# A two-layer diffusion block on one core: the late modulation sums at a chunk's end moved behind its last tail, two value tiles turned later, and the pairs' copies reordered

## The chip, the cores and the metric

The kernel runs on one core of a Trainium2 chip. The metric is the device time of one execution in microseconds (us). Five engines work side by side, each through its own list of instructions in a fixed order: TensorE (PE in the profile), VectorE (DVE), ScalarE (ACT), GpSimd (POOL) and SyncE (SP). Here POOL and SP mostly issue DMA transfers. An instruction that has to wait holds up everything behind it on its engine.

## The reference

Two layers over 512 latent tokens and 256 context tokens, width 1024. Layer 0 has latent attention and two-dimensional neighbourhood attention side by side, layer 1 grouped-query attention in a sliding window. Each attention and each feed-forward block reads a modulated, normalised stream, and its result goes back through a gate. The modulation vectors are products of a condition vector with a large matrix:

```python
for l in range(DEPTH):
    sh_a, sc_a, g_a, sh_f, sc_f, g_f = jnp.split(silu_c @ mod_w[l] + mod_b[l], 6, axis=-1)
    ...
    a_lat = modulate(h_lat, sh_a, sc_a)
    ...
    h_lat = h_lat + g_a * o_lat
    h_lat = h_lat + g_f * swiglu(modulate(h_lat, sh_f, sc_f), ffn_w_gate_up[l], ffn_w_down[l])
    if ctx_out:
        h_ctx = h_ctx + cg_a * o_ctx
        h_ctx = h_ctx + cg_f * swiglu(modulate(h_ctx, csh_f, csc_f), ffn_w_gate_up[l], ffn_w_down[l])
return rms_norm(h_lat, final_norm)
```

`swiglu` is `(silu(g) * u) @ w_down` with `g, u` the halves of `h @ w_gate_up`; the hidden width is 2816, which is 22 panels of 128.

## The kernel before, in words

Every 32-bit product is made of three TensorE products of split operands: each operand has a head (`wh`, `h`) and a remainder (`wl`, `lo`), and `mm3` and `product` issue head by head, head by remainder, remainder by head. A weight tile is loaded into `wr` by SP (L134), cast to `wh` by ACT (L309, L1518) and its remainder `wl` is made on the DVE (L311, L1519). Activations are kept with 128 features on the partitions and 768 tokens (512 latent, 256 context) along the row.

**The feed-forward block of layer 0** goes through the 22 hidden panels in chunks of four, four, four, four, four and two (`CHUNKS`, numbered 0 to 5). A panel is a `Pair`: `head`, `body` and `tail` are groups of products (a seven-product scheme for the four of a gate and an up panel), and its weights are split on the DVE at L1555 to L1565 and L1519. In the program the head of a pair comes ahead of the tail of the pair before. After the chunk's last tail, which makes the hidden tile `hs[3]` (L1594, then its split by L1518 and L1519), the chunk's down product runs over eight output tiles m = 0 to 7 (`down0`): it loads the residual tile m from memory (`fetched`, L1345, a transfer that POOL issues: `p<-home`), multiplies the weights by the four hidden tiles into two PSUM banks (latent and context part), adds the products to the residual tile on the DVE (L1341) and stores the tile (L1713, POOL: `home<-p`). The buffers of tag `p` hold these residual tiles, among others; there are eight.

PSUM has eight banks, three with tag `s`, two `t`, two `d`, one `o`. `PG` hands them out in the order s, t, s, d, t, s, d, so in the profile `pss`, `pst`, `psd` name the bank of a product. A product that begins a new use of a bank waits for the last reader of the use before, in the down product for an L1341.

**The late modulation sums.** Layer 1's modulation vectors are computed during layer 0's feed-forward, a tile at a time (`late_mods`): POOL fetches a 128 x 1024 weight tile into the only `rope0` buffer (L263), and the DVE multiplies it with the condition vectors and sums (L274, one or two instructions a tile). `late_step(place)` issues the sums of the tile that has been fetched, not ahead of the instruction `place`, and then the fetch of the next tile, which needs the buffer and so waits for the sums. `LATE` says how many such steps go with each pair and each output tile.

**What sets the order.** The program's text gives the order of issue, but a scheduler with its own costs then orders each engine's list; `behind(a, b)` makes it keep a behind b. So moving one step in the text can move others.

**Two other places.** In layer 0's attention `split_pair` takes the raw queries and keys of a neighbourhood pair apart into heads and remainders for two heads; halves of 64 partitions are moved by SP's copies (`t1[up] <- t0[dn]` and so on; L134). In layer 1, `VS` gets the values with tokens on the partitions: six transposes (L1771), four of latent and two of context tiles, of `v32` (made by ACT, L770), and copies. They run among the products of `swa_queries(1)` to `swa_queries(6)`.

## Time and profile before

| | before |
|---|---|
| time, median of 3 runs | 1530.44 us (1529.15 to 1530.89) |
| profiled execution: time, span | 1530.38 us, 1528.6 us |
| granted TensorE clock | 0.998 of full speed |
| busy: PE, DVE, ACT, POOL | 1512.8, 1177.6, 759.9, 194.8 us |
| chain that ended last: PE, DVE, all others | 91%, 5%, 4% |
| DMA | 225.94 MB, mean 148 GB/s |

How to read the rows. A row of the time-line begins with the start of an instruction (or of a run of like ones) and its duration in us, then engine, line, operation, `out<-in` by tile names without their numbers, the shape, and in brackets how long its engine stood idle before it and what ended that. A DMA row shows the time of its issue on the engine that issues it; when it lands is another view.

### The profile page before, as it was taken

The numbers are of one execution on the slowest core, as the hardware profiler recorded it, in microseconds if no ns is written. First come the engines' busy times: TensorE is split into PE (matmuls) and PEld (weight loads), VectorE is DVE, ScalarE is ACT, GpSimd is POOL, SyncE is SP. The second block draws the span as 40 slices with busy tenths as digits, with TensorE's granted clock in tenths as the row PEclk, the third lists the DMA queues.
The fourth block names the chain that finished last, engine by engine and source line by source line (L and its number), as shares of the span: only waits on it lengthen the run. The fifth ranks groups of instructions, "written<-read, shape, count | busy, mean of one in ns | idle before, by whom it ended". The sixth has DMA issues, their size and how long they took to land.

```text
span 1528.6 us, 26556 instructions
## 1 busy us (share of the span) xinstructions
PE 1512.8 (99%) x10008; PEld 1366.8 (89%) x10008; DVE 1177.6 (77%) x2427; ACT 759.9 (50%) x1531; POOL 194.8 (13%) x266
## 2 busy tenths in 40 slices
PE   9999999999999999999999999999999999999997
PEld 7788887889998998999999998888789999899897
DVE  4799877786876786877768677799977779678685
ACT  5533776684654242432424335567857455355353
POOL 0022210000111102012021122460011000000001
PEclk9999999999999999999999999999999999999999
DMA  9675753244733636547375494110224224324232
GB/s 337 242 226 183 182 126 98 58 148 151 234 125 108 232 102 218 183 144 286 122 259 182 151 369 141 60 38 1 98 82 140 84 79 136 104 83 131 90 97 84
DMA packets 80929, 225.94 MB, mean 148 GB/s; under 512 B 11232, under 2 KB 18400, under 8 KB 80800
## 3 DMA queue, kind: packets, MB, share of 16 engines
q1 hardware_dynamic: 61968, 148.73, 30.3%
q0 software_dynamic: 17680, 73.94, 14.2%
q8 instruction: 78, 1.28, 0.3%
q10 hardware_dynamic: 1152, 1.57, 0.3%
q14 instruction: 51, 0.42, 0.1%
HBM read 186.97 MB, written 23.07 MB: 137 GB/s over the span
## 4 chain that ended last, share of the span: by engine, by line
PE 91%; DVE 5%; ACT 1%; issue 1%; DMA 1%; POOL 0%; DVEq 0%; SPq 0%; ACTq 0%; POOLq 0%
PE pss L1532 5%; PE pss L1531 5%; PE pss L1533 5%; PE pss L346 4%; PE pss L349 4%; PE pss L348 4%; PE pso L576 4%; PE psd L346 4%; PE psd L348 4%; PE psd L349 4%; PE pst L346 3%; PE pst L348 3%; PE pst L349 3%; PE pst L1533 3%; PE pst L1532 3%; PE pst L1531 3%
## 5 line engine op out<-in xcount | busy, mean ns | idle before, releaser
L309 ACT CAST wh<-wr 128x512 fp32r<-128x512 f32 (+2 forms) x141 | 109.1, 787 | 211.3 <-DMA wr<-in_w_dn_dram 39.5
L311 DVE TENSOR_TENSOR wl<-wr,wh 128x512 fp32r<-128x512 f32 (+2 forms) x138 | 123.2, 899 | 87.9 <-ACT wh L309 83.5
L583 ACT ACTIVATE p<-p,sm 128x512 f32<-128x512 f32 (+3 forms) x144 | 105.1, 731 | 30.2 <-DVE sm L587 29.4
L1531 PE MATMUL pss<-b,wh 128*128 128x384 f32 (+1 forms) x346 | 107.8, 311 | 0.0
L1532 PE MATMUL pss<-b,wh 128*128 128x384 f32 (+1 forms) x346 | 107.7, 311 | 0.0
L1533 PE MATMUL pss<-b,wl 128*128 128x384 f32 (+1 forms) x346 | 107.2, 311 | 0.0
L274 DVE CUSTOM_DVE_ANT_0 p<-rope,cond 128x1024 bf16<-128x1024 f32 x64 | 78.0, 1219 | 10.6 <-DMA rope<-in_mod_w_dram 10.4
L348 PE MATMUL psd<-b,wh 128*128 128x512 f32 (+2 forms) x245 | 85.3, 348 | 0.0
L576 PE MATMUL pso<-ph,b 128*64 128x256 f32 (+1 forms) x400 | 77.8, 351 | 0.4 <-DVE ph L521 0.4
L576 PE MATMUL pso<-pl,b 128*64 128x256 f32 (+1 forms) x400 | 76.8, 351 | 0.0
L346 PE MATMUL psd<-b,wh 128*128 128x512 f32 (+2 forms) x206 | 75.5, 366 | 0.1
L349 PE MATMUL psd<-b,wl 128*128 128x512 f32 (+2 forms) x206 | 74.6, 362 | 0.0
L1518 ACT CAST wh<-wr 128x1024 fp32r<-128x1024 f32 x39 | 41.0, 1052 | 60.3 <-PE pss L348 15.2
L1531 PE MATMUL pst<-b,wh 128*128 128x384 f32 (+1 forms) x226 | 70.6, 312 | 0.0
L1532 PE MATMUL pst<-b,wh 128*128 128x384 f32 (+1 forms) x226 | 70.5, 312 | 0.0
L1533 PE MATMUL pst<-b,wl 128*128 128x384 f32 (+1 forms) x226 | 70.4, 312 | 0.0
L1518 ACT CAST wh<-pl 128x512 fp32r<-128x512 f32 x78 | 45.1, 619 | 48.5 <-PE pss L1532 21.1
L348 PE MATMUL pss<-b,wh 128*128 128x256 f32 (+2 forms) x215 | 68.9, 320 | 0.0
L346 PE MATMUL pss<-st,wh 128*128 128x512 f32 (+2 forms) x195 | 66.5, 341 | 0.2 <-ACT wh L309 0.2
L349 PE MATMUL pss<-st,wl 128*128 128x256 f32 (+2 forms) x195 | 66.5, 341 | 0.0
L1532 PEld LDWEIGHTS pss<-b,wh 128*128 128x128 f32 x346 | 65.0, 188 | 0.6 <-DVE wl L1519 0.4
L1531 PEld LDWEIGHTS pss<-b,wh 128*128 128x128 f32 x346 | 65.0, 188 | 0.6 <-issue 0.4
(712 smaller groups left out, 5221.4 us busy)
## 6 DMA issues: line engine op xcount, KB each, us to landing
wr<-in_w_gu_dram SPq DMA_DIRECT2D x88, 512.0 KB, 4.1
rope<-in_mod_w_dram POOLq DMA_DIRECT2D x48, 512.0 KB, 3.8
wr<-in_w_dn_dram SPq DMA_DIRECT2D x73, 256.0 KB, 2.8
wr<-in_w_out_dram SPq DMA_DIRECT2D x32, 512.0 KB, 3.6
p<-home POOLq DMA_DIRECT2D x40, 384.0 KB, 6.1
home<-p POOLq DMA_DIRECT2D x40, 384.0 KB, 5.5
wr<-in_w_in_dram SPq DMA_DIRECT2D x21, 512.0 KB, 3.9
ph<-in_mod_w_dram SPq DMA_DIRECT2D x24, 256.0 KB, 3.1
```

What stands on the lines that cost most here:

```text
L274: behind(V.tensor_tensor_reduce(out=unused, in0=w, in1=cond[:, v, :], op0=ALU.mult, op1=ALU.add, scale=1.0, scalar=0.0, accum_out=MOD[l, c ...
L309: behind(S.copy(h, r), *after[:1])
L311: behind((G if eng else V).tensor_tensor(lo, r, f(h), op=ALU.subtract), *after[1:])
L346: ins = PE.matmul(o, wh[:, k], mh[:, c], start=first and k == 0, stop=False)
L348: PE.matmul(o, wh[:, k], ml[:, c], start=False, stop=False)
L349: marks["product"] = PE.matmul(o, wl[:, k], mh[:, c], start=False, stop=last and k == n - 1)
L576: ins = PE.matmul(o[64 * i : 64 * i + 64, c], v(kt), t, start=n == 0, stop=n == len(moving[i]) - 1)
L583: S.activation(p[:, c], p[:, c], AF.Exp, bias=nm, scale=-1.0, accum_out=dn)
L1518: S.copy(h, t)
L1531: behind(PE.matmul(o, wh, xh, start=first and k == 0, stop=False, skip_group_check=not first), *after)
L1532: PE.matmul(o, wh, xl, start=False, stop=False, skip_group_check=not first)
L1533: ins = PE.matmul(o, wl, xh, start=False, stop=k == 3, skip_group_check=not first)
```

## The change

Three edits, in the text of the kernel.

1. In `ffn`, for layer 0 and the last pair of a chunk, the one late step that stood behind the pair's body is now behind its tail, and its sums may not be ahead of the tail's last split. This concerns chunks 1 to 4.
2. The transposes of the two context tiles into `VS` are issued after the steps that `swa_queries(2)` brings, behind the last product issued by then.
3. In `split_pair` the copy `t1[up] <- t0[dn]` is issued ahead of the subtraction that makes `lo`, and the two copies of a key tile's upper half onto its lower half come after all four copies into the second head's tiles.

```diff
@@ split_pair
         t0, t1 = sets[p][0]
         S.copy(t0[:, :NT], q)
         lo = q.bitcast(F32R)
+        behind(dma(t1[up, :NT], t0[dn, :NT]), *placed)
         low = V.tensor_tensor(lo, q, f(t0[:, :NT]), op=ALU.subtract)
         up_low(2, low)
         yield
-        behind(dma(t1[up, :NT], t0[dn, :NT]), *placed)
         dma(t1[dn, :NT], lo[dn])
         dma(t0[dn, :NT], lo[up])
...
         for x, y in ((h0, h1), (l0, l1)):
             dma(y[up, :NT], x[dn, :NT])
-            dma(y[dn, :NT], x[dn, :NT])
-            placed[:] = [dma(x[dn, :NT], x[up, :NT])]
+            placed[:] = [dma(y[dn, :NT], x[dn, :NT])]
+        for x in (h0, l0):
+            behind(dma(x[dn, :NT], x[up, :NT]), *placed)
         yield
@@ ffn
-            hs, last = [], None
+            hs, last, held_back = [], None, False
...
                     p.body()
                     hs.append(p.dst)
                     last = p
-                    if more(j) > 0:
+                    held_back = l == 0 and j == k0 + kc - 1 and more(j) > 0
+                    if more(j) > 0 and not held_back:
                         late_step(p.done)
...
             elif last:
                 last.tail()
+            if held_back:
+                late_step(last.done)
@@ layer 1
-    for t0, n in ((0, 4), (4, 2)):
+
+    def swa_values(t0, n, *after):
         o = PS("t")
         for i in range(n):
-            PE.transpose(o[:, i * P : (i + 1) * P], v32[:, (t0 + i) * P : (t0 + i + 1) * P], ident)
+            behind(PE.transpose(o[:, i * P : (i + 1) * P], v32[:, (t0 + i) * P : (t0 + i + 1) * P], ident), *after)
         copy(VS[:, t0 * P : (t0 + n) * P], o[:, : n * P])
+
+    swa_values(0, 4)
...
     for p in range(1, 7):
         beside(swa_queries(p))
...
+        if p == 2:
+            drain(side_work[0])
+            step(3)
+            swa_values(4, 2, marks["product"])
```

In the lists that follow, lines of the changed kernel are one to four higher than before (L1341 becomes L1342, L1345 L1346, L1713 L1717). Names carry their numbers.

SP at the copies of pair 3, where `st_2103` and `st_2104` are the query heads' tiles, `st_2105` to `st_2108` the keys' and `p_1646` is `lo`; before:

```order
L134 DMA b_1857<-b_1857 64x768
L134 DMA b_1858<-b_1858 64x768
L134 DMA st_2104<-st_2103 64x768
L134 DMA st_2104<-p_1646 64x768
L134 DMA st_2107<-st_2105 64x768
L134 DMA st_2103<-p_1646 64x768
L134 DMA st_2107<-st_2105 64x768
```

and now:

```order
L134 DMA b_1857<-b_1857 64x768
L134 DMA st_2104<-st_2103 64x768
L134 DMA b_1858<-b_1858 64x768
L134 DMA st_2104<-p_1646 64x768
L134 DMA st_2103<-p_1646 64x768
L134 DMA st_2107<-st_2105 64x768 x2
```

The first query copy moves ahead by one place, and the two copies from `p_1646` stand together.

POOL at the end of chunk 2, where `home_4240` to `home_4244` are residual tiles 0 to 4 in memory and each `p` the tile in the chip; before:

```order
L1345 DMA p_7409<-home_4240 128x768
L263 DMA rope_1532_7369<-in_mod_w_dram 128x1024
L1345 DMA p_7444<-home_4241 128x768
L1345 DMA p_7481<-home_4242 128x768
L263 DMA rope_1540_7442<-in_mod_w_dram 128x1024
L1713 DMA home_4240<-p_7409 128x768
L1713 DMA home_4241<-p_7444 128x768
L1345 DMA p_7522<-home_4243 128x768
L1345 DMA p_7559<-home_4244 128x768
L1713 DMA home_4242<-p_7481 128x768
```

and now:

```order
L1346 DMA p_7409<-home_4240 128x768
L263 DMA rope_1535_7407<-in_mod_w_dram 128x1024
L1717 DMA home_4240<-p_7409 128x768
L1346 DMA p_7444<-home_4241 128x768
L1346 DMA p_7481<-home_4242 128x768
L263 DMA rope_1540_7442<-in_mod_w_dram 128x1024
L1717 DMA home_4241<-p_7444 128x768
L1717 DMA home_4242<-p_7481 128x768
L1346 DMA p_7522<-home_4243 128x768
L1346 DMA p_7559<-home_4244 128x768
```

The loads of tiles 1 and 2 stand behind the store of tile 0, and those of tiles 3 and 4 behind the stores of tiles 1 and 2. Chunks 3 and 4 read the same with other numbers.

The DVE a little later in the same chunk, where `p_7522` and `p_7559` are tiles 3 and 4, and L1555 to `pl_7747` split the next pair's weights; before:

```order
L311 TENSOR_TENSOR wl_7686<-wr_7683,wh_7685 128x512
L1341 SCALAR_TENSOR_TENSOR p_7522<-pss_7524,mod_1136_5144,p_7522 128x512
L1341 SCALAR_TENSOR_TENSOR p_7522<-psd_7525,mod_1137_5145,p_7522 128x256
L1341 SCALAR_TENSOR_TENSOR p_7559<-pst_7561,mod_1136_5144,p_7559 128x512
L1341 SCALAR_TENSOR_TENSOR p_7559<-pss_7562,mod_1137_5145,p_7559 128x256
L1555 TENSOR_TENSOR pl_7730<-wr_7719 128x512
L1557 TENSOR_TENSOR ph_7731<-pl_7730,wr_7718 128x512
L1561 TENSOR_TENSOR ph_7736<-wr_7718,wr_7719 128x512
L1519 TENSOR_TENSOR wl_7723<-wr_7718,wh_7722 128x1024
L1565 TENSOR_TENSOR pl_7742<-wr_7718,ph_7731 128x512
L1519 TENSOR_TENSOR pl_7747<-wr_7719,ph_7746 128x512
```

and now:

```order
L1556 TENSOR_TENSOR pl_7730<-wr_7719 128x512
L1558 TENSOR_TENSOR ph_7731<-pl_7730,wr_7718 128x512
L1562 TENSOR_TENSOR ph_7736<-wr_7718,wr_7719 128x512
L1566 TENSOR_TENSOR pl_7742<-wr_7718,ph_7731 128x512
L1520 TENSOR_TENSOR wl_7723<-wr_7718,wh_7722 128x1024
L1520 TENSOR_TENSOR pl_7747<-wr_7719,ph_7746 128x512
L1342 SCALAR_TENSOR_TENSOR p_7522<-pss_7524,mod_1136_5144,p_7522 128x512
L1342 SCALAR_TENSOR_TENSOR p_7522<-psd_7525,mod_1137_5145,p_7522 128x256
L1342 SCALAR_TENSOR_TENSOR p_7559<-pst_7561,mod_1136_5144,p_7559 128x512
L1342 SCALAR_TENSOR_TENSOR p_7559<-pss_7562,mod_1137_5145,p_7559 128x256
```

The residuals of tiles 3 and 4 stand behind the six weight splits. The residuals of tiles 1 and 2 (not shown) moved likewise behind the L311 of tile 6's weights.

## The prediction

> **What bounds the kernel now.** I read the page's first part, then the time-line of each engine around the places that the change touches. The page's head and its busy times:

> ```profile
> span 1528.6 us, 26556 instructions
> PE 1512.8 (99%) x10008; PEld 1366.8 (89%) x10008; DVE 1177.6 (77%) x2427; ACT 759.9 (50%) x1531; POOL 194.8 (13%) x266
> ```

> TensorE runs its products in a fixed order and is busy for 99% of the span. The number of products does not change (only places in the order do), so the time can change only by waits: those that vanish from TensorE's row, and new ones. Each part below is therefore one question: what does TensorE wait for there now, and what after?

> **Part 3, the pairs' copies: about -0.7 us.** SP's time-line around pair 3, then the DVE instruction and the product that wait:

> ```profile
> 173.86 0.54 SPq L134 DMA_DIRECT2D st<-st  x1
> ...
> 181.51 0.46 SPq L134 DMA_DIRECT2D st<-p  x1
> ```
> ```profile
> 187.82 0.69 DVE L587 CUSTOM_DVE_ANT_0 p<-pss,b 128x512 f32<-128x512 f32 x1 [2.29 <-PE pss L778]
> ```
> ```profile
> 188.58 0.39 PE L777 MATMUL pss<-b,b 128*128 128x256 f32 x1 [0.78 <-DVE sm L587]
> ```

> The last `st<-p` copy reads `lo`, a tile with tag `p`; L587 writes its next row into a tile with that tag, and it starts at 187.82 although the DVE has been free for 2.29. (The row names a product; I take the copy, issued 6.3 us before, to be what ends last.) That copy could not be issued before the `st<-st` of 173.86 had landed, since it overwrites the half that this one reads. The change issues that `st<-st` one row earlier on SP (a row there takes about 0.5 us) and drops the row between the two `st<-p` copies. So the chain moves forward by 0.5 us at least, and at most the whole 0.78 of the product's wait goes. I take 0.7. If the copies don't move, the gain is 0.

> **Part 1 at chunk 1's end: about -0.9 us.** DVE's time-line, then the product:

> ```profile
> 592.97 1.23 DVE L274 CUSTOM_DVE_ANT_0 p<-rope,cond 128x1024 bf16<-128x1024 f32 x1 [0.79 <-DMA rope<-in_mod_w_dram]
> ...
> 595.05 1.22 DVE L274 CUSTOM_DVE_ANT_0 p<-rope,cond 128x1024 bf16<-128x1024 f32 x1
> ...
> 596.67 1.22 DVE L1519 TENSOR_TENSOR b<-p,b 128x384 fp32r<-128x384 f32 x2
> ```
> ```profile
> 596.30 0.27 PE L346 MATMUL pst<-b,wh 128*128 128x256 f32 x1
> 597.27 0.39 PE L348 MATMUL pst<-b,wh 128*128 128x256 f32 x1 [0.70 <-DVE b L1519]
> ```

> Two sums of 1.2 us each, the first after 0.79 of waiting for its weights, stand ahead of the split (L1519) of the chunk's last hidden tile, for which the first down product waits. The product before it began at 596.30; these two follow each other in 0.12 where nothing waits (a 256-column product, by the rows of this place), so 0.85 is lost. With the sums behind the split, the split comes some 2 us earlier: the wait goes, -0.9. The products that use the last hidden tile wait for nothing new here, as chunk 1's first three `home` loads are issued ahead of the rope fetch in either order.

> **The rest of the order: -0.3 and 0.** Three waits of TensorE, at the last chunk, at layer 1's value tiles, and 19 us behind these:

> ```profile
> 933.08 0.40 PE L349 MATMUL psd<-st,st 128*128 128x512 f32 x1
> 933.65 0.50 PE L346 MATMUL pst<-st,nb 128*128 128x512 f32 x1 [0.17 <-ACT st L1518]
> ```
> ```profile
> 979.35 0.44 PE L1771 MATMUL pst<-ident_r,b 128*128 128x128 f32 x2 [0.45 <-ACT b L770]
> ```
> ```profile
> 998.08 0.28 PE L777 MATMUL pss<-st,st 128*128 128x256 f32 x1
> 998.46 0.50 PE L346 MATMUL psd<-b,wh 128*128 128x512 f32 x1
> ```

> At 933.65 the scheduler now puts eight more products in front of the waiting one; the distance to the product before it is 0.57 us, of which a 512-column product needs some 0.23, and the rest goes: -0.3. At 979.35 the transposes of the context tiles wait for L770; ten products later (10 x 0.23 = 2.3 us) they don't, which is worth 0.45 to 0.62. But the product at 998.46, the first of a new psd bank, starts 0.38 after its neighbour and follows an ACT, DVE and POOL chain that does not wait for these transposes. What TensorE gains at 979 it waits for at 998: I take 0 and keep -0.6 as the other end.

> Gains together: 0.7 + 0.9 + 0.3 = 1.9 us.

> **Part 1 at the ends of chunks 2, 3 and 4: about +9.6 us.** Here the same move reorders POOL's queue. POOL's time-line at chunk 2, and what the loads took there:

> ```profile
> 683.00 1.08 POOL L1345 DMA_DIRECT2D p<-home  x2
> ...
> 692.95 0.55 POOL L1713 DMA_DIRECT2D home<-p  x1 [0.22 <-issue]
> 695.20 0.55 POOL L1713 DMA_DIRECT2D home<-p  x1 [1.71 <-DVE p L1341]
> 695.74 1.08 POOL L1345 DMA_DIRECT2D p<-home  x2
> ```
> ```profile
> DMA to landing us min/median/max: 4.2/5.5/7.3
> ```

> Before, the loads of residual tiles 1 and 2 go out at 683.00, far ahead. After, they stand behind the fetch that waits for the late sum, and behind the store of tile 0, which waits for tile 0's residual (issued at 692.95 here). They go out at about 693 and land, by the row's 4.2 to 7.3, at 697 to 700. The DVE follows suit; its time-line before, and two products:

> ```profile
> 693.77 0.74 DVE L1341 SCALAR_TENSOR_TENSOR p<-pss,mod,p 128x512 f32<-128x512 f32 x1
> ...
> 698.99 0.69 DVE L311 TENSOR_TENSOR wl<-wr,wh 128x512 fp32r<-128x512 f32 x1 [1.15 <-ACT wh L309]
> ...
> 702.62 0.75 DVE L1341 SCALAR_TENSOR_TENSOR p<-pss,mod,p 128x512 f32<-128x512 f32 x1 [0.17 <-DMA p<-home]
> ...
> 706.58 0.69 DVE L1555 TENSOR_TENSOR pl<-wr 128x512 f32<-128x512 f32 x1 [1.77 <-DMA wr<-in_w_gu_dram]
> ...
> 710.86 1.22 DVE L274 CUSTOM_DVE_ANT_0 p<-rope,cond 128x1024 bf16<-128x1024 f32 x1
> ```
> ```profile
> 699.61 0.28 PE L346 MATMUL pss<-st,wh 128*128 128x256 f32 x1
> ...
> 708.02 0.28 PE L346 MATMUL pss<-st,wh 128*128 128x256 f32 x1
> ```

> First wait. Tile 1's residual (693.77) moves behind the L311 of 698.99, which ends at 699.68; with 0.74 for itself it ends at 700.4. It frees the pss bank that the product at 699.61 (tile 4, third pss after it in the ring) begins: up to 0.8 us of waiting, none if the loads are quick and TensorE is late anyway.

> Second wait, the larger. The residuals of tiles 1 and 2 end near 702, so their stores and then the loads of tiles 3 and 4 go out near 702.5 instead of 695.74 and land at 707 to 710. In the DVE's new order the residual of tile 3 (702.62 now) stands behind the split of the next pair's weights, L1555 up to the row ahead of the L274 at 710.86. So it starts at 710.86 and ends at 711.6. It frees the bank of the pss product that begins at 708.02 (tile 6). That product begins 3.6 us late (the first wait is contained in this). The same two rows at chunks 3 and 4:

> ```profile
> 803.66 1.22 DVE L274 CUSTOM_DVE_ANT_0 p<-rope,cond 128x1024 bf16<-128x1024 f32 x1
> ```
> ```profile
> 800.45 0.28 PE L346 MATMUL pss<-st,wh 128*128 128x256 f32 x1
> ```
> ```profile
> 896.20 1.22 DVE L274 CUSTOM_DVE_ANT_0 p<-rope,cond 128x1024 bf16<-128x1024 f32 x1
> ```
> ```profile
> 892.87 0.28 PE L346 MATMUL pss<-st,wh 128*128 128x256 f32 x1
> ```

> 803.66 + 0.74 - 800.45 = 3.95 and 896.20 + 0.74 - 892.87 = 4.07. Sum 11.6 us, if the split of the weights stays where it is. That hangs on when the gate weights land: L1555 starts on their landing. Their transfer at chunk 2, the DMA share there, and the page's median for such loads:

> ```profile
> DMA to landing us min/median/max: 6.9/6.9/6.9
> ```
> ```profile
> DMA  9999999999979999999798999999999999999999
> ...
> DMA packets 698, 2.84 MB, mean 406 GB/s; under 512 B 101, under 2 KB 101, under 8 KB 698
> ```
> ```profile
> wr<-in_w_gu_dram SPq DMA_DIRECT2D x88, 512.0 KB, 4.1
> ```

> The engines are full there, so the load takes 6.9 and not 4.1. Its issue does not move (it follows the L311 of 698.99). After the change, two stores and two loads of 384 KB move from 695 to 697 to about 701 to 703, and two loads of that size come in at 693: some 0.4 to 0.8 MB less ahead of the gate weights, but as much more beside them. Lower end: 4.1, that is 2.8 us earlier, leaves 0.8, 1.2 and 1.3, together 3.3. Upper end: the 0.79 MB that used to land at 683 to 688 is now in the full stretch, which moves 406 GB/s, so 1.9 us more at each chunk: 11.6 + 5.7 = 17.3 in all. I take 0.65 off each wait, near the measured row: 2.9 + 3.3 + 3.4 = 9.6.

> [...]

> **The sum.** The profiled execution took 1530.38 us (span 1528.6 and 1.8 around it), 0.06 under the median of 1530.44. 1530.4 - 1.9 + 9.6 = 1538.1 us.

> **The rivals.**
> - Light: the gate weights land in 4.1 us, and the waits shrink to 3.3 in all: 1530.4 - 1.9 + 3.3 = 1531.8. For it: the page's median. Against it: the stretch was full at all three chunks.
> - Hidden, the other side: the residual of tile 3 never holds TensorE. The point that decides: the gate weights landing within 6.9 - 3.6 = 3.3 us of their issue, and tile 3's load by then too. Then only gains are left: 1530.4 - 1.9 = 1528.5, and 1527.9 with the 0.6 of the value tiles kept. Against it: 3.3 is below the page's median for that load.
> - Crowded: POOL's late loads also delay the weights: up to 1530.4 - 1.9 + 17.3 = 1545.8.
> - The value tiles do nothing: this is in the sum already, as a gain eaten 19 us later.

> **How the numbers follow.** A measurement of this kernel tells about 0.2%, 3.1 us, from no change: the lines are 1527.4 and 1533.5. Forecast (each of the three waits 2 us or more): 0.62. Crowded: 0.10. Light: 0.17. Hidden: 0.11, of which 0.03 falls below 1527.4, as the runs shown reach 1.3 us under their median. So slower 0.72, same 0.25, faster 0.03. The range takes in the light case and part of the crowded one: 1530.5 to 1544.0.

> **What would show it.** In the profile after: at chunks 2, 3 and 4, POOL issues `home<-p` ahead of `p<-home x2`, and those loads start some 9 us later than 683.00. Among TensorE's waits a row "pss L346 <- DVE p L1341" appears, three times or more, with a longest of about 3 us, and is the largest of the list. The wait of L348 for L1519 at 597 is gone, that of L777 for L587 near 188 is shorter, that of L1771 for L770 is gone, and one at 998 is longer. The forecast is wrong if the bank of the product at 708 is freed by something that I have not seen moved earlier, or if the gate weights land before 704.

## The result, and the profile after

The changed kernel takes 1546.04 us (median of 5 runs, 1545.33 to 1549.35) against 1530.51 before (5 runs). The ratio is 1.0103, interval 1.0091 to 1.0115: 1% slower. The prediction said 1538.1, range 1530.5 to 1544.0. The direction was right, and so were the chunk ends that lose. The size was not: the change moved the time by 15.5 us, and 7.7 were forecast.

The page's head and busy times of the changed kernel, to set beside those of before:

```profile
span 1544.3 us, 26547 instructions
PE 1518.7 (98%) x10008; PEld 1370.2 (89%) x10008; DVE 1179.2 (76%) x2427; ACT 759.8 (49%) x1531; POOL 194.3 (13%) x266
```

TensorE has the same 10008 products and 15.7 us more of span. The list of TensorE's waits over the whole execution (line waited for, us in total, times, longest), after:

```profile
PE pss L346 <- DVE p L1342: 7.8, 6, 2.3
PE psd L1532 <- DVE p L1342: 2.5, 3, 1.7
PE psd L937 <- DVE ones L166: 1.1, 1, 1.1
PE pst L346 <- ACT st L1519: 1.0, 1, 1.0
```

Before, no wait for a residual (L1341, now L1342) was in that list. Now nine of them make 10.3 us, three at each of chunks 2, 3 and 4. POOL's time-line at chunk 2:

```profile
691.87 0.55 POOL L1717 DMA_DIRECT2D home<-p  x1 [2.20 <-DVE p L1342]
692.41 1.07 POOL L1346 DMA_DIRECT2D p<-home  x2
694.82 0.54 POOL L263 DMA_DIRECT2D rope<-in_mod_w_dram  x1 [1.34 <-DVE mod L274]
699.44 0.54 POOL L1717 DMA_DIRECT2D home<-p  x1 [4.08 <-DVE p L1342]
701.09 0.54 POOL L1717 DMA_DIRECT2D home<-p  x1 [1.11 <-DVE p L1342]
701.63 1.07 POOL L1346 DMA_DIRECT2D p<-home  x2
```

The loads of tiles 1 and 2 went out at 692.41 instead of 683.00, those of tiles 3 and 4 at 701.63 instead of 695.74, each pair behind a store that waits for a residual. The DVE there (residuals of tiles 1, 3 and 5, and the first weight split):

```profile
698.00 0.75 DVE L1342 SCALAR_TENSOR_TENSOR p<-pss,mod,p 128x512 f32<-128x512 f32 x1 [0.73 <-DMA p<-home]
...
704.59 0.69 DVE L1556 TENSOR_TENSOR pl<-wr 128x512 f32<-128x512 f32 x1
...
708.87 0.74 DVE L1342 SCALAR_TENSOR_TENSOR p<-pss,mod,p 128x512 f32<-128x512 f32 x1
...
718.66 0.75 DVE L1342 SCALAR_TENSOR_TENSOR p<-psd,mod,p 128x512 f32<-128x512 f32 x1 [0.31 <-DMA p<-home]
```

The products that waited for their banks, from three windows of TensorE's time-line:

```profile
698.81 0.39 PE L346 MATMUL pss<-st,wh 128*128 128x256 f32 x1 [0.50 <-DVE p L1342]
```
```profile
709.67 0.39 PE L346 MATMUL pss<-st,wh 128*128 128x256 f32 x1 [2.16 <-DVE p L1342]
709.89 0.28 PE L348 MATMUL pss<-st,wh 128*128 128x256 f32 x1
710.00 0.28 PE L349 MATMUL pss<-st,wl 128*128 128x256 f32 x1
...
710.80 0.41 PE L348 MATMUL pss<-b,wh 128*128 128x256 f32 x1
711.02 0.41 PE L349 MATMUL pss<-b,wl 128*128 128x256 f32 x1
711.23 0.41 PE L346 MATMUL pss<-b,wh 128*128 128x256 f32 x1
```
```profile
719.47 0.44 PE L1532 MATMUL psd<-b,wh 128*128 128x384 f32 x1 [0.30 <-DVE p L1342]
```

The middle fence shows something that the trace of before did not have between 4.62 and 1523.55 us, where its granted clock was 1.00. Products of 256 columns follow each other in 0.11 us at 709.9, and in 0.21 to 0.22 from 710.6 on: behind the wait TensorE falls to half speed. The clock that the trace records is at half from 710.33 to 713.74. The same stretch with granted clock (seventh figure after the window, PEclk), before and after:

```profile
710.00:720.00 10.00, 10.00 (x60) 9.55 (x59) 9.91 (x18) 3.80 (x7) 2.17 (x4) 1.00 0.70 230
```
```profile
710.00:720.00 10.00, 9.70 (x51) 8.64 (x50) 7.33 (x14) 3.38 (x6) 2.70 (x5) 0.83 0.88 311
```

0.83 over 10 us is 3.4 us at half speed, which costs half of that, 1.7 us; the distances of the products, added up, give 1.5.

Where the 15.5 us come from, by the start of the same product in both traces (how far the product has moved, median over windows of 20 us; a step in it is a loss or gain at that place):

| place | step, us | forecast |
|---|---|---|
| pair 3's copies, near 188 | -0.6 | -0.7 |
| chunk 1's end, near 597 | -1.0 | -0.9 |
| chunk 2's end | +5.4 | +2.9 |
| chunk 3's end | +5.2 | +3.3 |
| chunk 4's end and the last chunk | +5.8 | +3.4 and -0.3 |
| layer 1 | +0.5 | 0 |

Of the 0.5 in layer 1, 0.1 is at the value tiles. The rest comes in two small steps behind 1200 us; e8 and e9 below, which leave part 2 out, lose 0.5 and 0.4 in layer 1 as well, so it is not put down to part 2.

### The profile page after: what moved, and what is told of

Its sections match the earlier page's. It is cut to its first block, busy times and chain, and to the rows that moved or that the text cites. A ratio compares the mean times of both kernels' runs of the same rounds, so it can differ in the third digit from the quotient of the medians.

```text
span 1544.3 us, 26547 instructions
## 1 busy us (share of the span) xinstructions
PE 1518.7 (98%) x10008; PEld 1370.2 (89%) x10008; DVE 1179.2 (76%) x2427; ACT 759.8 (49%) x1531; POOL 194.3 (13%) x266
## 4 chain that ended last, share of the span: by engine, by line
PE 86%; DVE 6%; DMA 4%; ACT 2%; issue 1%; POOL 1%; SPq 0%; DVEq 0%; ACTq 0%; POOLq 0%
PE pss L1533 5%; PE pss L1532 5%; PE pss L1534 5%; PE pso L576 4%; PE pss L346 4%; PE pss L348 4%; PE pss L349 4%; PE psd L346 4%; PE psd L348 4%; PE psd L349 4%; PE pst L1534 3%; PE pst L1532 3%; PE pst L1533 3%; PE pst L346 3%; PE pst L348 3%; PE pst L349 3%
## 5 line engine op out<-in xcount | busy, mean ns | idle before, releaser
L309 ACT CAST wh<-wr 128x512 fp32r<-128x512 f32 (+2 forms) x141 | 109.2, 787 | 210.5 <-PE psd L348 40.8
L311 DVE TENSOR_TENSOR wl<-wr,wh 128x512 fp32r<-128x512 f32 (+2 forms) x138 | 123.1, 900 | 89.3 <-ACT wh L309 85.0
L274 DVE CUSTOM_DVE_ANT_0 p<-rope,cond 128x1024 bf16<-128x1024 f32 x64 | 78.1, 1221 | 12.1 <-DMA rope<-in_mod_w_dram 11.7
L348 PE MATMUL psd<-b,wh 128*128 128x512 f32 (+2 forms) x245 | 85.3, 348 | 0.0
L346 PE MATMUL psd<-b,wh 128*128 128x512 f32 (+2 forms) x206 | 75.6, 367 | 0.1
L346 PE MATMUL pss<-st,wh 128*128 128x256 f32 (+2 forms) x195 | 67.5, 346 | 8.0 <-DVE p L1342 7.8
L349 PE MATMUL psd<-b,wl 128*128 128x512 f32 (+2 forms) x206 | 74.7, 362 | 0.5 <-DVE wl L311 0.5
L1519 ACT CAST wh<-wr 128x1024 fp32r<-128x1024 f32 x39 | 41.0, 1052 | 64.2 <-PE pss L348 16.1
L348 PE MATMUL pss<-b,wh 128*128 128x256 f32 (+2 forms) x215 | 69.4, 323 | 0.0
L1519 ACT CAST wh<-pl 128x512 fp32r<-128x512 f32 x78 | 44.8, 619 | 47.4 <-PE pss L1533 23.4
L349 PE MATMUL pss<-st,wl 128*128 128x256 f32 (+2 forms) x195 | 66.9, 343 | 0.0
L1520 DVE TENSOR_TENSOR wl<-pl,wh 128x512 fp32r<-128x512 f32 x78 | 50.9, 688 | 20.4 <-ACT wh L1519 20.2
L1533 PEld LDWEIGHTS pss<-b,wh 128*128 128x128 f32 x346 | 65.0, 188 | 0.6 <-DVE wl L1520 0.4
## 6 DMA issues: line engine op xcount, KB each, us to landing
wr<-in_w_gu_dram SPq DMA_DIRECT2D x88, 512.0 KB, 4.0
rope<-in_mod_w_dram POOLq DMA_DIRECT2D x48, 512.0 KB, 3.9
wr<-in_w_out_dram SPq DMA_DIRECT2D x32, 512.0 KB, 3.6
wr<-in_w_in_dram SPq DMA_DIRECT2D x21, 512.0 KB, 3.9
```

Source lines behind the costliest of these rows:

```text
L274: behind(V.tensor_tensor_reduce(out=unused, in0=w, in1=cond[:, v, :], op0=ALU.mult, op1=ALU.add, scale=1.0, scalar=0.0, accum_out=MOD[l, c ...
L309: behind(S.copy(h, r), *after[:1])
L311: behind((G if eng else V).tensor_tensor(lo, r, f(h), op=ALU.subtract), *after[1:])
L346: ins = PE.matmul(o, wh[:, k], mh[:, c], start=first and k == 0, stop=False)
L348: PE.matmul(o, wh[:, k], ml[:, c], start=False, stop=False)
L349: marks["product"] = PE.matmul(o, wl[:, k], mh[:, c], start=False, stop=last and k == n - 1)
```

## The experiments

"L" in the expectations is the theory of late loads, "D" that of the DVE's order.

**e1 and e2: which part it is.** e1 sets `held_back = False` in the changed kernel; e2 is the kernel before with the `ffn` hunks of the diff alone.

> The change without its part 1: late sums at a chunk's end stay behind the body, value tiles and copies as changed. Theory L (all of the loss comes from part 1, which puts POOL's loads of residual tiles 1 to 4 behind the held-back fetch and the stores): only the copies' gain stays, 0.6 us by the trace of the changed kernel, so about 1529.9 us and no wait of a pss product for a residual. Rival V (parts 2 or 3 lose something of their own, at layer 1): 1531 us or more.

> The kernel before with part 1 alone. Theory L: -1.0 us at chunk 1's end and +16.4 us at the ends of chunks 2, 3 and 4 (5.4, 5.2 and 5.8 in the trace of the changed kernel), so about 1545.9 us. Rival V: clearly less than 1545.

Measured: e1 1529.97 us (11 runs), ratio 0.9991 (0.9982 to 1.0000). e2 1549.72 us (4 runs), ratio 1.0117 (1.0103 to 1.0131). Part 1 alone makes the whole loss, and 3.8 us more than the 1545.9 that were expected. From 640 to 930 us every engine of e2 works through the same list as in the changed kernel, so the excess is one of timing and not of order: its waits for residuals make 13.0 us where those of the whole change made 10.3, its granted clock was 0.994 beside 0.995, and the first wait at chunk 2 was 2.3 us long there. Rival V is out.

**e3: part 1 at chunk 1 only.**

```diff
-                    held_back = l == 0 and j == k0 + kc - 1 and more(j) > 0
+                    held_back = l == 0 and j == 7
```

> The change with part 1 at chunk 1's end only; at chunks 2, 3 and 4 the sums stand behind the body as before. Theory L: POOL's order at chunks 2 to 4 is the old one, the gains of 0.6 (copies) and 1.0 (chunk 1) stay: about 1528.9 us, some 0.1% under the kernel before. Rival C (the gain at chunk 1 is given back later, as the last chunk's waits take it): 1529.9 us.

Measured: 1529.37 us (11 runs), ratio 0.9987 (0.9978 to 0.9996). The loss is at chunks 2 to 4 alone. The time lies between L's 1528.9 and the 1529.9 of rival C. In this trace 1.1 us of the gain is lost again at the last chunk, where ACT got a weight tile later; e8, whose lists are the same up to there, did not lose it, so that is one execution and not the order.

**e4: five loads ahead.**

```diff
             if held_back:
+                homes[:] = [fetched(m, slice(0, NT)) for m in range(5)]
                 late_step(last.done)
...
-        t = fetched(m, slice(0, NT))
+        t = homes.pop(0) if homes else fetched(m, slice(0, NT))
```

> The whole change, and at a chunk's end the loads of residual tiles 0 to 4 are issued ahead of the held-back sums and their fetch; in the DVE's list the residuals of tiles 3 and 4 then stand ahead of the next pair's weight splits again. Theory L: the waits at chunks 2 to 4 and the slow stretches of TensorE behind them go, 1529 us, give or take 1. Rival S (the held-back sums themselves cost the time, as they stand on the DVE ahead of the first residuals): some 1 us a chunk stays, 1532 us or more.

Measured: 1543.96 us (5 runs), ratio 1.0076 (1.0063 to 1.0089). Theory L's number did not come. The time is in the range of rival S (1532 us or more), but not for its reason: most of the loss stayed, at another place. The waits for tiles 1 to 4 are gone; TensorE's longest wait at chunk 2 is now for the residual of tile 5 (its waits from 690 to 735, and the DVE):

```profile
PE psd L1532 <- DVE p L1342: 3.2, 1, 3.2
```
```profile
714.58 0.69 DVE L1556 TENSOR_TENSOR pl<-wr 128x512 f32<-128x512 f32 x1 [2.00 <-DMA wr<-in_w_gu_dram]
...
717.11 0.74 DVE L1342 SCALAR_TENSOR_TENSOR p<-psd,mod,p 128x512 f32<-128x512 f32 x1
```

Tile 5's load had landed at 710.5. Its residual stood behind the weight splits of the second following pair, which themselves waited for their load until 714.58. The row ahead of it names that load, and not the held-back sums, so the time does not show rival S.

**e5 and e6: loads and DVE order apart.** e5 keeps POOL's changed order and puts the residuals of tiles 3 and 4 ahead of the next pair's splits:

```diff
+        if m == 4:
+            marks["fifth"] = ins
...
+            fifth = [marks.pop("fifth")] if "fifth" in marks else []
-            behind(V.tensor_tensor(s1, u[:, h[0]], u[:, h[1]], op=ALU.add), *self.after,
+            behind(V.tensor_tensor(s1, u[:, h[0]], u[:, h[1]], op=ALU.add), *self.after, *fifth,
```

> The whole change, and each chunk's first following pair splits its weights behind the residual of tile 4, so the DVE's order of tiles 3 and 4 is the old one; POOL's order stays the changed one. Theory L (late loads): in the trace of the changed kernel tile 3's load landed at 708.72 and the splits ended at 708.87, so the residual starts only 0.15 us earlier and the waits stay near 2.2 us: 1545 to 1546 us. Theory D (the DVE's order alone makes the second wait): those waits go, with the slow stretches behind them some 10 us: about 1536 us.

e6 is e4 with `range(3)`: tiles 0 to 2 are loaded ahead, and tile 3's residual stays behind the splits.

> The whole change, and at a chunk's end the loads of tiles 0 to 2 are issued ahead of the held-back sums; tile 3's residual still stands behind the next pair's weight splits on the DVE. Theory L: the loads of tiles 3 and 4 go out some 5 us sooner and the waits go: 1530 us. Theory D: the first wait (0.4 to 0.7) goes, the second, at tile 6's pss product, stays at 2 us or more at each of the three chunks: 1542 to 1546 us.

Measured: e5 1549.28 us, ratio 1.0114 (1.0094 to 1.0133); e6 1548.93 us, ratio 1.0113 (1.0099 to 1.0127), 4 runs each. In e5, POOL and then the DVE at chunk 2:

```profile
702.12 1.07 POOL L1346 DMA_DIRECT2D p<-home  x2
```
```profile
706.37 1.22 DVE L1520 TENSOR_TENSOR wl<-wr,wh 128x1024 fp32r<-128x1024 f32 x1 [2.03 <-ACT wh L1519]
707.62 0.75 DVE L1342 SCALAR_TENSOR_TENSOR p<-pss,mod,p 128x512 f32<-128x512 f32 x1
...
709.85 0.75 DVE L1342 SCALAR_TENSOR_TENSOR p<-pst,mod,p 128x512 f32<-128x512 f32 x1 [1.08 <-DMA p<-home]
```

The residual of tile 3 ran 0.02 us after its load had landed (707.60). One of the six splits, which the edit does not hold back, ended at the same moment (706.37 and 1.22), so this place alone does not tell the two apart. Chunks 3 and 4 do; there the DVE was idle for 1.3 and 1.9 us until the load of tile 3 landed:

```profile
809.35 0.75 DVE L1342 SCALAR_TENSOR_TENSOR p<-pss,mod,p 128x512 f32<-128x512 f32 x1 [1.33 <-DMA p<-home]
```
```profile
906.09 0.75 DVE L1342 SCALAR_TENSOR_TENSOR p<-pss,mod,p 128x512 f32<-128x512 f32 x1 [1.91 <-DMA p<-home]
```

With the splits out of its way, the load held the residual alone, and the product of tile 6 still waited 0.4, 1.7 and 2.3 us at the three chunks. Theory D's 1536 is out. The edit made the next pair's splits late as well, which brought new waits of 3.3 and 4.6 us in the profiled execution, so the whole time of e5 is not a measure of late loads; the four runs are 1546.0, 1546.6, 1552.0 (the profiled one) and 1552.2. In e6 the load went out at 697.04 and landed at 704.07:

```profile
697.04 1.07 POOL L1346 DMA_DIRECT2D p<-home  x2
```
```profile
706.04 0.69 DVE L1556 TENSOR_TENSOR pl<-wr 128x512 f32<-128x512 f32 x1 [1.92 <-DMA wr<-in_w_gu_dram]
...
710.31 0.75 DVE L1342 SCALAR_TENSOR_TENSOR p<-pss,mod,p 128x512 f32<-128x512 f32 x1
```
```profile
PE pss L346 <- DVE p L1342: 3.6, 1, 3.6
```

The residual ran 6.2 us after its load had landed, straight behind the splits: here the DVE's order held it alone. L's 1530 is out. The time is 3 us above D's range; the granted clock was 0.83 from 710 to 720, and 0.66 from 805 to 815 and from 905 to 915. That is five intervals of 3.4 us at half speed; the changed kernel's trace has two at its chunk ends (last section). So late loads and the DVE's order are both right, and either alone is enough for a wait at tile 6's product. In the changed kernel they meet: the load of tile 3 landed at 708.72, the splits ended at 708.87.

**e7: both undone.** e4, and the second following pair splits its weights behind the residual of tile 6 (the same edit as in e5, with a list that holds the last instructions of tiles 4 and 6).

> Five loads ahead as in e4, and the second following pair splits its weights behind the residual of tile 6. In e4 the residual of tile 5 stood behind those splits, 6.6 us after its load had landed, and TensorE waited 3.3 us for it. If late loads and the DVE's order are the whole loss: no wait over 1 us at the ends of chunks 2 to 4, 1529 to 1530 us. If the held-back sums cost by themselves, or the wait moves on once more: 1533 us or more.

Measured: 1532.14 us (11 runs), ratio 1.0006 (0.9997 to 1.0015). Some 14 of the 15.5 us are gone with the sums still held back at all four chunks. The time lies between the two that were expected. What is left at chunk 2:

```profile
PE psd L1532 <- DVE p L1342: 0.6, 1, 0.6
```

A wait of this size stands at each of chunks 2, 3 and 4, and the granted clock was 0.998 of full speed, as in the kernel before. Between starts of products the three make 2.2 us, and the last chunk another 0.8, of the 3.5 us that this trace still loses from chunk 2 on against before. That shows the cause of the rest: loads behind stores on POOL, and residuals behind splits on the DVE. It also shows that holding the sums back gains nothing at chunks 2 to 4: there was no wait to remove there.

**e8 to e11: what the small parts are worth.** e8 is e3 without part 2, e9 part 3 alone, e10 part 1 at chunk 1 alone, e11 the kernel before once more.

> Part 1 at chunk 1's end only and part 3, without part 2 (the value tiles are turned where they were). If part 2 is worth nothing, as its gain is waited for 19 us later: the same as e3, 1529.4 us within 0.5. If part 2 gives its 0.6: about 1530.0. If it costs, as the extra steps behind swa_queries(2) move layer 1's work: under 1529.

> The kernel before with part 3 alone. Theory P (the new order of the copies takes the wait near 188 away): 0.6 to 0.8 us under the kernel before. Rival N (when those copies land differs from execution to execution, and the order of the issues gives nothing that can be told): e2, without part 3, also had only 0.2 us of that wait in its trace; then the same as before within 0.1%.

> The kernel before with part 1 at chunk 1's end only, without parts 2 and 3. If the gain there is 1.0 us as in the traces: 1.0 us (0.07%) under the kernel before, and e8 (with part 3) another 0.6 or more below it if theory P holds, no further if rival N holds.

> The kernel before itself, as a second profiled execution and to see what this comparison tells from no change: ratio 1.000 within 0.1%; the wait near 188 anywhere from 0 to 0.8 us by rival N, 0.7 to 0.8 again by theory P.

| | us, median | runs | ratio, interval |
|---|---|---|---|
| e8, chunk 1 and copies | 1528.97 | 11 | 0.9980 (0.9970 to 0.9990) |
| e9, copies | 1530.69 | 11 | 0.9986 (0.9977 to 0.9995) |
| e10, chunk 1 | 1529.14 | 11 | 0.9985 (0.9977 to 0.9994) |
| e11, before again | 1531.51 | 12 | 1.0005 (0.9993 to 1.0016) |

The kernel before had a median of 1531.5 in these comparisons. e9 and e10 each gain 0.14 to 0.15% of it by the ratio, some 2 us (by the medians 0.8 and 2.4), with intervals that just exclude 1. e8, with both, is the fastest kernel here, 0.2% under the kernel before and 1.1% under the changed one, but its interval overlaps those of e9, e10 and e3, so that the two gains add up is not shown. On part 2 the difference of e3 and e8 says nothing either.

The wait near 188 was 0.8 and 1.2 us in the two traces of the kernel before, 0.2 and 0.5 in e2 and e10 (old order of the copies as well), and 0 to 1.0 in the nine traces with part 3 (mean 0.2, against 0.7 without). So it differs by execution with either order; that part 3 makes it smaller is likely, from e9's time and these means, and not shown by single traces. The wait at 597 is clear: 0.7 and 1.0 in before, 1.3 in e1, 0.3 in e9, and none in any of the kernels with part 1 at chunk 1.

## Why the prediction was wrong, step by step

The sum of the forecast had two waits at each chunk end, and took a wait to cost the time in which TensorE stands still. What failed is that it stopped there: a third wait, the clock behind two of the waits, and the loss at the last chunk are 6.6 us for which it had nothing or a small gain.

- **POOL's order (right).** The store of tile 0 at 691.87, the loads at 692.41 and 701.63: forecast 693 and 702.5.
- **The first and second wait together (right, a little high).** Between the starts of products, the two waits added up to 0.66 + 2.33 = 3.0 us at chunk 2, 0.39 + 2.48 = 2.9 at chunk 3 and 0.38 + 2.51 = 2.9 at chunk 4: 8.8 us, where the term was 9.6. One reason given was wrong: the gate weights' load did move, from 699.71 to 697.30, since the L311 that it follows ran at 696.58 and not at 698.99; it took 6.8 us (6.9 before). So the splits ended 2.0 us sooner than worked out. TensorE itself was 1.5 us ahead of before at this place (-0.6 and -1.0 in the table), so 0.5 of it counts, near the 0.65 that was taken off for another reason: that near agreement is luck. At that moment the load of tile 3 was the other half of the wait. The time of the gate weights' load hardly changed (6.8 beside 6.9 us), while the load ahead of it on SP's queue took 8.1 us (693.41 to 701.52) beside 6.0 before (695.53 to 701.49). What POOL had queued was not varied by itself, so how its backlog bears on these loads was not shown.
- **The third wait (missed, 3.0 us).** I followed the chain from tile 1 to tile 3 and stopped. It goes on: the stores of tiles 3 and 4 were late, so the loads of tiles 5 and 6 were, and the next pair's first psd product waited for tile 5's residual: 0.46, 1.87 and 0.63 us between starts, for which the sum had nothing.
- **Half speed after a wait (missed, 2.8 us).** 1.5 us at chunk 2 and 1.3 at chunk 4. The forecast counted a wait as the time in which TensorE stands still. With these two waits the clock fell as well: 0.83 from 710 to 720 and from 900 to 910. The wait at chunk 3 is as long (2.31 us, beside 2.16 and 2.35), and the clock stayed at 1.00 from 800 to 820; the last section sets the three side by side.
- **The last chunk (wrong, +0.8 us).** Forecast -0.3; TensorE's wait for ACT there is 1.0 us and was 0.2. It is 1.0 in all six traces with part 1 at every chunk, and at most 0.7 in the seven others, so it comes with part 1 at chunks 2 to 4; by which step is not shown.
- The rest of the 16.4 us of the three chunk ends, about 1.0 us, is not itemised: the first product behind a wait takes 0.1 us longer, nine times.
- **The value tiles (right in size, the place off).** The wait at 979 is gone, and one of 0.5 us for L311 came at 994, 4 us ahead of where it was expected. Together they are a loss of 0.1.
- **The range.** "Crowded" gave 1545.8 and a tenth of the chance, and the range stopped short of it. The time came out there for other reasons than that case names: the gate weights' loads did not become slower (6.8, 6.4 and 6.3 us at the three chunks, 6.9, 6.7 and 7.3 before), there were more waits than I had counted. The range took in errors in the terms that I had, and nothing for terms that I hadn't found.

## What to carry to other kernels

A step that is moved behind a late result carries its DMA issue along, and everything that stands behind that issue in its queue (here the loads of tiles 1 and 2, from 683.00 to 692.41). Read the queue to its end: who waits for each transfer, and which engine's list holds the waiting instruction; here it took both lists to undo the loss. And where TensorE is the bound engine, a wait can cost more than its length: here the clock was at half for 3.4 us with waits of 2.16 and 2.35 us, and for 6.8 us with four of the five waits of 3.2 to 4.4 us in e4 and e6.

## What the hardware showed that was not expected

| trace, place | wait, us | granted clock | at half speed, us |
|---|---|---|---|
| changed kernel, chunk 2 | 2.16 | 0.83 (710 to 720) | 3.4 |
| changed kernel, chunk 3 | 2.31 | 1.00 (800 to 810) | 0 |
| changed kernel, chunk 3, third wait | 1.71 | 1.00 (810 to 820) | 0 |
| changed kernel, chunk 4 | 2.35 | 0.83 (900 to 910) | 3.4 |
| e4, chunk 2 | 3.2 | 0.84, 0.82 (710 to 720, 720 to 730) | 6.8 |
| e4, chunk 3 | 3.8 | 0.79, 0.87 (810 to 820, 820 to 830) | 6.8 |
| e6, chunk 2 | 3.6 | 0.83 (710 to 720) | 3.4 |
| e6, chunk 3 | 4.4 | 0.66 (805 to 815) | 6.8 |
| e6, chunk 4 | 3.8 | 0.66 (905 to 915) | 6.8 |

In the changed kernel at chunk 2, TensorE ran at full speed for 0.66 us behind the wait before the half speed began (from 709.67 to 710.33 above). At chunk 4 the clock had already fallen, at 904.89, when the wait ended at 905.02.

The length alone does not sort the waits of the changed kernel: that of 2.16 us was followed by half speed, that of 2.31 us was not. Where they lie in time differs. The granted clock of this trace changes at 710.33, 713.74, 904.89 and 908.30, and once more at 1536.35. From the first to the second it is 3.413 us, from the second to the third 191.15, 56 times 3.413, and from the fourth to the last 628.05, 184 times 3.413. Cut into such intervals, these are the stretches around the wait of 2.16 us at chunk 2 and the longer one of 2.31 us at chunk 3 (PE's busy time is the second figure, the clock the seventh again):

```profile
706.92:710.33 3.41, 1.25 (x8) 0.81 (x7) 3.41 (x6) 0.00 (x0) 0.03 (x1) 1.00 0.91 334
710.33:713.74 3.41, 3.41 (x14) 3.02 (x13) 3.01 (x6) 1.14 (x2) 2.12 (x4) 0.50 0.97 381
```
```profile
802.49:805.90 3.41, 2.59 (x12) 1.74 (x10) 3.38 (x6) 1.28 (x2) 0.37 (x1) 1.00 1.00 384
805.90:809.31 3.41, 1.92 (x14) 1.88 (x15) 3.01 (x6) 0.26 (x1) 0.73 (x2) 1.00 1.00 353
809.31:812.73 3.42, 3.42 (x21) 2.93 (x20) 3.28 (x6) 1.50 (x3) 1.95 (x4) 1.00 0.99 344
```

The first wait lies in one interval and leaves 2.16 of its 3.41 us idle; the next interval runs at half speed. The second is parted at 805.90 into 0.82 and 1.49 us, and the clock stays. From 25 us to TensorE's last products this sorts every interval at full clock of two traces, of the kernel before (counted back from its change of clock at 1523.55) and of the changed one: with 1.49 us idle or less the next one ran at full clock (874 intervals), with 2.16 and 2.21 us at half (2). The two intervals at half speed, with 0.13 us idle or less, were each followed by one at full clock. What lies between these figures is not shown here.
